# The second layer's modulation summed in one PSUM bank, with the FFN's gating and low parts on GpSimd

## The chip, the cores and the metric

The kernel runs on one core of one Trainium2 chip. The metric is the device time of one execution in microseconds (us), as the median of several runs. The core's engines are TensorE (PE in the profile; PEld is its loading of weights), VectorE (DVE), ScalarE (ACT), GpSimd (POOL) and SyncE (SP), which here issues the DMAs. Each engine works through its own instructions in order, and waits on semaphores for the others.

## What is computed

The reference is one inference step of a small diffusion backbone: two layers, width 1024, with 128 context tokens and 1024 latent tokens. The inner dimension of the FFN is 2816. What matters for this change is the modulation and the FFN:

```python
for i in range(DEPTH):                                   # 2 layers
    mc = split(silu(c_ctx) @ w_mod[i] + b_mod[i], 6)     # context stream
    ml = split(silu(c)     @ w_mod[i] + b_mod[i], 6)     # latent stream
    h  = rmsnorm(x, norm_mix[i]) * (1 + m[1]) + m[0]
    x  = x + m[2] * mixer_i(h)      # layer 0: attention and pooling, layer 1: convolution module
    h  = rmsnorm(x, norm_ffn[i]) * (1 + m[4]) + m[3]
    x  = x + m[5] * conv_ffn(h)

def conv_ffn(h, w_in, conv_w, conv_b, w_out):
    a, g = split(dwconv3(h @ w_in, conv_w, conv_b), 2)
    return (silu(a) * g) @ w_out
```

`m` is `mc` for the context tokens and `ml` for the latent ones. The six modulation vectors of a layer are a product of two vectors of length 1024 with a matrix of 1024 x 6144, 25 MB that are read once and used for very little arithmetic. Everything is in float32.

## The kernel before

**Layout and precision.** Activations stand feature-major: eight tiles `xs[k]` of 128 features by 1154 columns (128 context tokens, 2 of gap, 1024 latent tokens). A large product is made of three matmuls in the faster float32r: each operand is split in a high part and a low part (the value less its high part), and `mm3` adds high x high, high x low and low x high into the same PSUM tile. A weight unit (`wunit`, L242) is a DMA of 512 KB into `wraw`, a high part `whi` by ACT (L252) and a low part `wlo` by Pool (L254). The two raw buffers and the three buffers each of `whi` and `wlo` are used in turn. While layer 0's first FFN part runs, its low parts are also stored in DRAM, and its second part loads them from there.

**Stages.** After attention (`mixer0`) comes `trunk`. The tokens are cut in two parts, about 664 and 492 columns wide, and the stages follow one another so that each part's vector work lies beside the other's matmuls. The wider part takes two matmuls per 128 x 128 weights (332 columns each), the other takes one. The order in `trunk` is:

1. the output projection of layer 0 on part OA (`out_tiles`, eight tiles, the first three together), then on part OB;
2. layer 0's FFN on part FA0, then on part FB0;
3. layer 1's convolution module, beside FB0 and after it;
4. layer 1's FFN on FA1 and FB1.

**What is done beside the matmuls** is written as generators. Each `yield` ends a step, and `pull(q, n)` or `tick(n)` runs steps from the list between the pieces of the main loop. In OA, `pull(mods, MS)` runs four steps of the modulation after each of its six yields. In OB, `tick(3)` runs the norm for FA0, and no modulation (`MT` is 0). In FA0, `tick(MO)` runs 1.1 steps after each yield, first of the norm for the other part (17 steps), then what is left of the modulation. A planner with a timeline of expected times then sets the order of the instructions on each engine, SP and its DMA queue included.

**The modulation of layer 1** (`mod_beside`, L309) is a matrix-vector product for two streams done by DVE, for three groups m of two vectors each. For each of eight row blocks k and each of four column chunks of 512 it loads a tile `mraw` of 256 KB, multiplies it by the stream's 128 scalars (one per partition) and adds it into one of eight accumulators `modacc` in SBUF, four for each stream (L322 for k = 0, L324 for the others). So there are 32 steps of two operations each, one for each stream, and then a step in which eight matmuls with a column of ones (L330) sum over the partitions into the PSUM tile `modps`, and a step in which `mod_spread` (L336) copies it, turns it into columns and adds the bias. That is 34 steps a group, 102 in all. There are eight buffers of `mraw`.

**The FFN** (`ffn`, L1076) goes through 22 pairs of a projection a and a projection g. `conv` (L1087) empties the PSUM tile with a three-tap convolution: ACT (L1091), then DVE twice (L1092, L1094). `pair` then takes the Silu of a, multiplies by g (L1104) and splits the product in high (`fh`, ACT, L1107) and low (`fl`, L1108). After each two pairs `out` (L1112) runs the output projection for eight tiles d, each with a residual add by DVE (L437, in `residual`), in four yields. It runs behind the first pair of the next two. The engine of L1104 and L1108 is chosen by whether a PSUM pool `psd` exists: with it Pool does both, without it DVE does L1108 and, for a part of two chunks, L1104.

**PSUM** has eight banks. From the start of `trunk` until the sixth yield of FB0 the pools are `psum(3, 0, 2)`: three tiles `mm` of two banks and two auxiliary banks. Later stages have the extra pool `psd`, in which the convolution of layer 1 (L996) accumulates.

The norm's chain is: squares by ACT (L402), added by DVE (L406), summed over partitions by TensorE (L380), `rsv` by DVE (L368), the power -1/2 `rsr` by Pool (L371), and a broadcast by TensorE (L392).

Of the kernel before, what the change touches and what calls it, by code (L numbers as in the profile page):

```python
# [9 lines left out]
F32 = mybir.dt.float32  # L10
F32R = mybir.dt.float32r
AF = mybir.ActivationFunctionType
ALU = mybir.AluOpType
# [6 lines left out]
P = 128  # L20
D = 1024
KT = D // P
# [94 lines left out]
FA1, FB1 = Part(0, 648), Part(642, T)  # L117
UW = 692
SIDE_A = 7
MO = 1.1  # L120
MS = 4
MT = 0
MI = 1.1
PF = (1, 3, 2, 0)
SEQ = (0, 0), (0, 1), (1, 0), (1, 1), (2, 0), (2, 1)
KP = 0
# [62 lines left out]
class Kern:  # L189
# [119 lines left out]
    def mod_beside(self, l, m, mp, ev):  # L309

        nc = self.nc
        accs = [mp.tile([P, 512], F32, tag="macc", name=self.nm("modacc")) for _ in range(8)]
        for k in range(KT):
            for u in range(2):
                for x in range(2):
                    rv = mp.tile([P, 512], F32, tag="mraw", name=self.nm("mraw"))
                    o = u * 1024 + x * 512
                    nc.sync.dma_start(rv, self.i["wmod"][l, m, k, :, o:o + 512])
                    for s in range(2):
                        acc, c = accs[4 * s + 2 * u + x], self.sc[:, k, s:s + 1]  # L320
                        if k == 0:
                            i = nc.vector.tensor_scalar(acc, rv, c, None, op0=ALU.mult)  # L322
                        else:
                            i = nc.vector.scalar_tensor_tensor(acc, rv, c, acc, op0=ALU.mult, op1=ALU.add)  # L324
                        self.tc.keep_in_program_order(i)
                    yield
        ps = self.psa.tile([P, 512], F32, tag="aux", name=self.nm("modps"))
        for s in range(2):
            for g in range(4):
                nc.tensor.matmul(ps[32 * g:32 * g + 32, :], self.one[:, 1 - s:33 - s], accs[4 * s + g],  # L330
                                 start=s == 0, stop=s == 1)
        yield
        self.mod_spread(l, m, ps, ev, self.psa, "aux")
        yield
# [911 lines left out]
    def trunk(self):  # L1246
        tc, nc, I, cp = self.tc, self.nc, self.i, self.cp
# [9 lines left out]

        with ExitStack() as st:
            pool = lambda n, b, **kw: st.enter_context(tc.tile_pool(name=n, bufs=b, reuse_waits="tile", **kw))
            self.psum(3, 0, 2)  # L1260
            st.callback(lambda: self.pstack.close())
            xp = pool("xp", 1)
            self.halo = xp.tile([P, KT, 32], F32, name="halo")
# [5 lines left out]
            hB = pool("hB", 16)  # L1269
            nt = pool("nt", 3)  # L1270
            beside = ExitStack()
            mp = beside.enter_context(tc.tile_pool(name="mp", bufs=8, reuse_waits="tile"))
            self.tw = 664
            xs = []
            for k in range(KT):
                x = xp.tile([P, T], F32, name=f"x_{k}")
# [7 lines left out]
            for part, Hc in ((OA, mkA()), (OB, mkB(OB.c0))):  # L1284
                Hc.order = order
                tiles = {}
                for k in order:
                    c = ft.tile([P, self.tw], F32, tag="ft", name=self.nm("cat"))
# [14 lines left out]
            for _ in self.out_tiles(OA, I["woab"], cat[OA], xs, self.mod(0, 2), 0, 664, first=3):  # L1303
                self.pull(mods, MS)
            gf0 = self.gain(0, 4, "nf0")
# [11 lines left out]
            for o in self.ffn(0, FA0, xs, HA, self.mod(0, 5), 0, 662, ft, None):  # L1317
                self.tick(MO if o else MI)
            self.flush(self.bg)
# [8 lines left out]
            accs = []  # L1328
# [30 lines left out]
            accs = []  # L1359
# [145 lines left out]
```

## Time and profile before

| what | us |
|---|---|
| median of three runs | 2699.41 |
| lowest and highest of them | 2694.0, 2701.53 |
| the profiled execution: time | 2696.8 |
| the profiled execution: span of the core | 2694.8 |

The mean granted clock of TensorE was 0.989 of full speed in the profiled execution. The page shows one execution. "Busy" is the time in which an engine ran an instruction of its own, "idle before" is the time that it stood still ahead of one, and "<-" names what it waited for. Row groups give the line of the kernel, the engine, the operation, the output and inputs by the program's names, the shape, the count after "x", and then busy time and mean ns of one. In a timeline, the first number is the start and the second the time from there to the end of the merged pieces; instructions are pipelined, so that the next one of an engine starts before the one ahead of it has wholly ended.

The modulation of layer 1 stands in the trace as 24 operations of L322 and 168 of L324 on DVE, from 541 to 1140 us, and 48 matmuls of L330.

### The profile page before, as it was taken

What the parts mean: (1) busy time and instruction counts of PE and PEld (TensorE: products, weight loads), DVE (VectorE), ACT (ScalarE), POOL (GpSimd) and SP (SyncE); (2) the same over time, 40 slices, a digit from 0 to 9 for tenths busy, and PEclk for the clock granted to TensorE, in tenths of its full rate; (3) what the DMA queues carried; (4) which work ended last, traced back from release to release, by engine and by line L of the source; (5) the groups of instructions that cost most, each with busy time, mean ns of one, the idle gap of its engine ahead of it and who ended that gap; (6) DMA issues with size and microseconds to landing.
All of it is one profiled execution on the core that took longest, in us unless ns stands there. A gap on an engine that the chain in (4) does not pass through costs nothing.

```text
span 2694.8 us, 38615 instructions
## 1 busy us (share of the span) xinstructions
PE 2605.4 (97%) x14982; PEld 2352.9 (87%) x14982; DVE 1597.6 (59%) x2455; ACT 1124.1 (42%) x1743; POOL 1244.9 (46%) x736
## 2 busy tenths in 40 slices
PE   6999998989999999999999999999999999999999
PEld 4698897788999999989998889889999999888887
DVE  6046777493567767654997854379964344444444
ACT  4326666525422222354545364555324323433332
POOL 1322333265433332233556254689757544655553
PEclk9999998999999999999999999999999999999999
DMA  7612235564446555444444553222222222433332
GB/s 283 221 51 79 71 79 142 184 198 135 139 161 205 190 172 179 170 160 141 141 133 133 187 188 102 87 87 76 73 71 71 79 80 70 129 93 95 95 96 89
DMA packets 139734, 345.88 MB, mean 128 GB/s; under 512 B 46112, under 2 KB 51872, under 8 KB 139552
## 3 DMA queue, kind: packets, MB, share of 16 engines
q1 hardware_dynamic: 139552, 343.41, 40.1%
q8 instruction: 119, 1.95, 0.3%
q14 instruction: 63, 0.52, 0.1%
HBM read 291.97 MB, written 46.67 MB: 126 GB/s over the span
## 4 chain that ended last, share of the span: by engine, by line
PE 82%; DVE 10%; ACT 2%; issue 2%; DMA 2%; POOL 1%; SPq 0%; POOLq 0%; DVEq 0%; ACTq 0%
PE mm L264 15%; PE mm L268 15%; PE mm L266 15%; PE mn L264 8%; PE mn L266 8%; PE mn L268 8%; PE mm L454 2%; DVE modacc L324 2%; DVE x L437 2%; PE O L888 2%; DVE dacc L996 1%; PE tp L856 1%; PE qps L638 1%; PE qps L639 1%; PE qps L640 1%
## 5 line engine op out<-in xcount | busy, mean ns | idle before, releaser
L254 POOL TENSOR_TENSOR wlo<-wraw,whi 128x1024 fp32r<-128x1024 f32 x280 | 687.7, 2462 | 909.3 <-ACT whi L252 737.6
L252 ACT ACTIVATE whi<-wraw 128x1024 fp32r<-128x1024 f32 x348 | 364.5, 1057 | 770.8 <-PE mm L266 396.4
L264 PE MATMUL mm<-h,whi 128*128 128x332 f32 (+6 forms) x2208 | 558.3, 323 | 7.1 <-DVE x L437 6.6
L268 PE MATMUL mm<-h,wlo 128*128 128x332 f32 (+6 forms) x2208 | 560.0, 324 | 0.9 <-POOL wlo L254 0.8
L266 PE MATMUL mm<-h,whi 128*128 128x332 f32 (+6 forms) x2208 | 558.6, 324 | 0.0
L264 PEld LDWEIGHTS mm<-h,whi 128*128 128x128 f32 x2208 | 382.6, 189 | 21.5 <-issue 8.6
L268 PEld LDWEIGHTS mm<-h,wlo 128*128 128x128 f32 x2208 | 381.0, 189 | 13.5 <-POOL wlo L254 1.9
L266 PEld LDWEIGHTS mm<-h,whi 128*128 128x128 f32 x2208 | 379.7, 189 | 10.4
L996 DVE SCALAR_TENSOR_TENSOR dacc<-u,params,dacc 128x661 f32<-128x661 f32 (+1 forms) x344 | 285.3, 829 | 7.6
L437 DVE SCALAR_TENSOR_TENSOR x<-mm,mod,x 128x128 f32<-128x128 f32 (+7 forms) x408 | 210.4, 559 | 130.8 <-PE mm L268 129.2
L264 PE MATMUL mn<-h,whi 128*128 128x494 f32 (+1 forms) x672 | 262.5, 391 | 3.2 <-DVE x L437 3.2
L266 PE MATMUL mn<-h,whi 128*128 128x494 f32 (+1 forms) x672 | 262.1, 390 | 0.0
L268 PE MATMUL mn<-h,wlo 128*128 128x494 f32 (+1 forms) x672 | 260.5, 390 | 0.0
L1092 DVE SCALAR_TENSOR_TENSOR facc<-mm,params,facc 128x663 f32<-128x663 f32 (+3 forms) x92 | 82.1, 892 | 275.0 <-ACT facc L1091 274.9
L1092 DVE SCALAR_TENSOR_TENSOR facc<-mn,params,facc 128x493 f32<-128x493 f32 (+1 forms) x84 | 62.0, 738 | 218.6 <-ACT facc L1091 218.5
L264 PE MATMUL mm<-fh,whi 128*128 128x332 f32 (+2 forms) x720 | 171.7, 318 | 14.2 <-DVE x L437 12.3
L268 PE MATMUL mm<-fh,wlo 128*128 128x332 f32 (+2 forms) x720 | 169.5, 315 | 0.0
L266 PE MATMUL mm<-fl,whi 128*128 128x332 f32 (+2 forms) x720 | 169.4, 315 | 0.0
L978 POOL TENSOR_TENSOR acc<-acc,tap 128x508 f32<-128x508 f32 (+1 forms) x104 | 151.3, 1460 | 38.6 <-ACT tap L977 32.6
L1104 POOL TENSOR_TENSOR facc<-facc,facc 128x494 f32<-128x494 f32 (+2 forms) x66 | 91.3, 1383 | 145.1 <-DVE facc L1094 145.1
L437 DVE SCALAR_TENSOR_TENSOR x<-mn,mod,x 128x510 f32<-128x510 f32 (+1 forms) x168 | 120.5, 736 | 63.8 <-PE mn L268 63.0
L1107 ACT ACTIVATE fh<-facc 128x664 fp32r<-128x664 f32 (+3 forms) x88 | 60.2, 684 | 227.5 <-POOL facc L1104 140.1
(227 smaller groups left out, 4539.1 us busy)
## 6 DMA issues: line engine op xcount, KB each, us to landing
wraw<-in_fi_dram SPq DMA_DIRECT2D x176, 512.0 KB
wraw<-in_fo_dram SPq DMA_DIRECT2D x88, 512.0 KB
mraw<-in_wmod_dram SPq DMA_DIRECT2D x48, 512.0 KB
mraw<-in_wmod_dram SPq DMA_DIRECT2D x96, 256.0 KB
wraw<-in_pw_dram SPq DMA_DIRECT2D x48, 512.0 KB
lowi<-wlo SPq DMA_DIRECT2D x44, 512.0 KB
wlo<-lowi SPq DMA_DIRECT2D x44, 512.0 KB
lowo<-wlo SPq DMA_DIRECT2D x22, 512.0 KB
```

Of the source, the lines that this page charges most:

```text
L252: nc.scalar.activation(hi, raw, AF.Copy)
L254: (eng or nc.gpsimd).tensor_tensor(lo, raw, hi.bitcast(F32), op=ALU.subtract)
L264: mm(pv, whi, xhi[:, a:b], start=start, stop=False)
L266: mm(pv, whi, xlo[:, a:b], start=False, stop=False)
L268: mm(pv, wlo, xhi[:, a:b], start=False, stop=stop)
L324: i = nc.vector.scalar_tensor_tensor(acc, rv, c, acc, op0=ALU.mult, op1=ALU.add)
L437: nc.vector.scalar_tensor_tensor(xd[:, a:b], pv, gate[:, d, st:st + 1], xd[:, a:b], op0=ALU.mult, op1=ALU.add)
L978: nc.gpsimd.tensor_tensor(acc[:, :n], acc[:, :n], p[:, :n], op=ALU.add)
L996: nc.vector.scalar_tensor_tensor(acc[:, :n] if t == NCK - 1 else pacc, u[:, t:t + n], wk(i, t), acc[:, :n] if t == side else pacc, op0=ALU ...
L1092: nc.vector.scalar_tensor_tensor(acc[:, 1:W], part.ps(ps, 0, W - 1), w(0), acc[:, 1:W], op0=ALU.mult, op1=ALU.add)
L1104: (nc.gpsimd if side or part.n == 1 else nc.vector).tensor_tensor(a[:, :W], a[:, :W], g[:, :W], op=ALU.mult)
L1107: nc.scalar.activation(hi[:, :W], a[:, :W], AF.Copy)
```

## The change

```diff
-MO = 1.1
-MS = 4
+MO = 1.3
+MS = 2
+MR = 11
 MT = 0
-MI = 1.1
+MI = 1.3
...
     def mod_beside(self, l, m, mp, ev):
 
         nc = self.nc
-        accs = [mp.tile([P, 512], F32, tag="macc", name=self.nm("modacc")) for _ in range(8)]
-        for k in range(KT):
-            for u in range(2):
-                for x in range(2):
-                    rv = mp.tile([P, 512], F32, tag="mraw", name=self.nm("mraw"))
-                    o = u * 1024 + x * 512
-                    nc.sync.dma_start(rv, self.i["wmod"][l, m, k, :, o:o + 512])
-                    for s in range(2):
-                        acc, c = accs[4 * s + 2 * u + x], self.sc[:, k, s:s + 1]
-                        if k == 0:
-                            i = nc.vector.tensor_scalar(acc, rv, c, None, op0=ALU.mult)
-                        else:
-                            i = nc.vector.scalar_tensor_tensor(acc, rv, c, acc, op0=ALU.mult, op1=ALU.add)
+        accs = [mp.tile([P, 512], F32, tag="macc", name=self.nm("modacc"), bufs=8) for _ in range(8)]
+        raws = []
+
+        def load():
+            n = len(raws)
+            if n < 4 * KT:
+                raws.append(mp.tile([P, 512], F32, tag="mraw", name=self.nm("mraw"), bufs=MR))
+                nc.sync.dma_start(raws[n], self.i["wmod"][l, m, n % KT, :, n // KT * 512:n // KT * 512 + 512])
+
+        for _ in range(MR):
+            load()
+        for g in range(4):
+            for s in range(2):
+                acc = self.psd.tile([P, 1, 512], F32, tag="acc", name=self.nm("macc"))[:, 0]
+                for k in range(KT):
+                    rv, c = raws[g * KT + k], self.sc[:, k, s:s + 1]
+                    if k == 0:
+                        nc.scalar.activation(acc, rv, AF.Identity, scale=c)
+                    else:
+                        i = nc.vector.scalar_tensor_tensor(accs[4 * s + g] if k == KT - 1 else acc, rv, c, acc,
+                                                           op0=ALU.mult, op1=ALU.add)
                         self.tc.keep_in_program_order(i)
-                    yield
+                    if s:
+                        load()
+                    if k % 2:
+                        yield
...
-            self.psum(3, 0, 2)
+            self.psum(3, 0, 1, 1)
...
-            mp = beside.enter_context(tc.tile_pool(name="mp", bufs=8, reuse_waits="tile"))
+            mp = beside.enter_context(tc.tile_pool(name="mp", bufs=1, reuse_waits="tile"))
```

- The eight sums of a group m are made one after the other: for each chunk g and each stream s, eight products over k. The running sum is in a PSUM bank of the pool `psd`, of which there is one. The last of the eight writes its result to the accumulator in SBUF, as before.
- The first product of each sum (24 in all) is by ACT, the other seven (168) by DVE.
- A step is two products of one sum, where it was one tile for both streams. There are still 32 such steps in a group, and the two that follow.
- A raw tile is used by both streams, eight products apart. Eleven tiles are loaded ahead, and the next is loaded after each product of the second stream. The 96 loads of 256 KB are the same data in another order, by chunk and not by row block.
- OA gets two steps per yield, 12 in all, and 90 are left for FA0, where 1.3 steps are run per yield.
- `psum(3, 0, 1, 1)` takes one of the two auxiliary banks for `psd`. Since `psd` then exists from the start of `trunk`, the FFN's product (L1104) and low part (L1108) are Pool's for the 22 pairs of FA0, and the low part of the first pair of FB0 as well.

## The prediction

> **What bounds the kernel now.** I read the top of the page first, then the windows cut at the stages that the change touches, then TensorE's waits inside them.
>
> ```profile
> span 2694.8 us, 38615 instructions
> PE 2605.4 (97%) x14982; PEld 2352.9 (87%) x14982; DVE 1597.6 (59%) x2455; ACT 1124.1 (42%) x1743; POOL 1244.9 (46%) x736
> PE 82%; DVE 10%; ACT 2%; issue 2%; DMA 2%; POOL 1%; SPq 0%; POOLq 0%; DVEq 0%; ACTq 0%
> ```
>
> TensorE sets the time: the chain runs through it for 82%. The change removes none of its matmuls, so a gain can only come out of its gaps. The chain also has 10% on DVE, and the next view says where DVE matters.
>
> ```profile
> core 0: us, PE busy (x) PEld busy (x) DVE busy (x) ACT busy (x) POOL busy (x), PEclk, DMA share, GB/s
> 517.00:578.50 61.50, 59.55 (x390) 58.79 (x389) 40.85 (x40) 15.18 (x21) 28.85 (x15) 1.00 0.69 237
> 578.50:640.00 61.50, 51.55 (x222) 43.24 (x221) 36.57 (x51) 27.75 (x49) 40.48 (x17) 0.92 0.47 154
> 640.00:1145.00 505.00, 494.93 (x3196) 482.53 (x3194) 331.28 (x462) 154.11 (x186) 171.30 (x75) 1.00 0.52 173
> ```
>
> The three stretches are the output projection of part OA, that of part OB, and the first FFN part FA0. In the middle one TensorE is busy for 51.55 of 61.50 us, at a granted clock of 0.92. FA0 has 10.07 us of gaps in 505. The waits of TensorE, first for 517 to 640 and then for 640 to 1145, name the cause:
>
> ```profile
> PE mm L264 <- DVE x L437: 6.6, 4, 2.4
> PE mm L392 <- POOL rsr L371: 4.0, 1, 4.0
> PE mm L268 <- POOL wlo L254: 0.8, 2, 0.5
> ```
>
> ```profile
> PE mm L264 <- DVE x L437: 10.0, 7, 2.1
> ```
>
> L437 is the residual add, which empties a PSUM tile and so frees it for the next matmuls. DVE reaches it late. The timeline of DVE in OA shows why:
>
> ```profile
> 541.44 11.77 DVE L322 TENSOR_SCALAR modacc<-mraw,sc 128x512 f32<-128x512 f32 x8
> ...
> 587.27 8.66 DVE L324 SCALAR_TENSOR_TENSOR modacc<-mraw,sc,modacc 128x512 f32<-128x512 f32 x8
> 595.85 0.84 DVE L406 TENSOR_TENSOR sq<-sq,sq 128x664 f32<-128x664 f32 x1
> 596.62 1.02 DVE L437 SCALAR_TENSOR_TENSOR x<-mm,mod,x 128x128 f32<-128x128 f32 x2
> ```
>
> Behind each tile's residual (the last row, two pieces) stand eight modulation operations, 8.66 and 11.77 us in the batches shown. A tile of OA takes TensorE 48 matmuls of 0.153 us (59.55 us in 390), 7.3 us. The queue falls behind in OA and is still paying in OB.
>
> **The change part by part.** *Fewer steps in OA.* Two steps for four per yield leaves a tile with one residual (1.02 us), one square add (0.84) and four modulation operations for eight. At 1.25 us a step (worked out below) these are 2.5 us, so 4.4 us in all, under the 7.3 us of the matmuls. DVE no longer trails, and what it held up in OB falls away:
>
> ```profile
> 587.50 0.46 PE L264 MATMUL mm<-h,whi 128*128 128x490 f32 x1 [1.47 <-DVE x L437]
> ...
> 590.41 0.61 PE L264 MATMUL mm<-h,whi 128*128 128x490 f32 x1
> 590.82 0.61 PE L266 MATMUL mm<-h,whi 128*128 128x490 f32 x1
> ...
> 593.23 0.38 PE L264 MATMUL mm<-h,whi 128*128 128x490 f32 x1
> 593.45 0.38 PE L266 MATMUL mm<-h,whi 128*128 128x490 f32 x1
> ```
>
> The terms: residual waits 6.6, a late low part 0.5 of the 0.8. Then the clock: soon after a wait the matmuls start every 0.41 us (590.41 to 590.82) where they start every 0.22 otherwise (593.23 to 593.45). The window's 0.92 on 61.5 us is some 4.9 us of clock, of which I count 3.0 for the two spells before 605 (eight matmuls each, 0.19 us too long). Together 10.1 us.
>
> The wait of 4.0 us for rsr is the same backlog by another way:
>
> ```profile
> 599.51 8.79 POOL L254 TENSOR_TENSOR wlo<-wraw,whi 128x1024 fp32r<-128x1024 f32 x2 [7.44 <-ACT whi L252]
> 611.83 2.35 POOL L254 TENSOR_TENSOR wlo<-wraw,whi 128x1024 fp32r<-128x1024 f32 x1 [3.53 <-ACT whi L252]
> 614.13 1.32 POOL L371 TENSOR_TENSOR rsr<-rsv,mhalf 128x6 f32<-128x6 f32 x1
> ```
>
> Two low parts take 8.79 us on Pool against 2.35 for one, while DVE runs the modulation. The next low part comes late by its high part (3.53), and rsr stands behind it in Pool's queue. With DVE idle there, I drop this wait too: 4.0. OA and OB give **14.1 us**.
>
> *The sums into PSUM.* From the per-line answers, with minimum, median and maximum in ns:
>
> ```profile
> L324 DVE SCALAR_TENSOR_TENSOR modacc<-mraw,sc,modacc x168: 732/743/2914, 555.8 to 1139.4; 128x512 f32<-128x512 f32 x168
> L996 DVE SCALAR_TENSOR_TENSOR dacc<-u,params,dacc x344: 734/898/912, 1267.3 to 1987.2; 128x661 f32<-128x661 f32 x88, 128x508 f32<-128x508 f32 x84
> L996 DVE SCALAR_TENSOR_TENSOR dacc<-u,params,acc x16: 868/1860/3050, 1265.3 to 1959.8; 128x661 f32<-128x661 f32 x8, 128x508 f32<-128x508 f32 x8
> ```
>
> The convolution's sums (L996) already accumulate in PSUM and never pass 912 ns, though Pool is often busy beside them; with both inputs in SBUF (acc) the same line reaches 3050, as the modulation reaches 2914. So the stretched ones go. The price is order: the new sums depend on each other. Six dependent PSUM sums take 4.68 us in the convolution, (4.68 - 0.74)/5 = 0.79 from start to start, against 0.66 for the independent ones now (the four from 832.48 to 835.13, below). A step of two then costs 1.45 (one dependent start, one covered by other work) for 1.32, and with the first of each eight on ACT 1.25 on average.
>
> ```profile
> 1860.84 4.68 DVE L996 SCALAR_TENSOR_TENSOR dacc<-u,params,dacc 128x508 f32<-128x508 f32 x6
> ```
>
> Both have 0.73 as the least, so the place itself is charged at nothing. The Trainium skill speaks against that (Perfetto Trace Analysis, Optimizing Scalar/DVE Operations): it charges DVE about 125 ns of access on PSUM and 60 on SBUF. By it each sum would cost 0.065 us more, an estimate, 0.6 us for the ten of an out section, and the sum would be 10 us for 16; the least of 732 and 734 ns doesn't bear it out.
>
> *Gating and low parts on Pool.* They leave DVE and come back slower on Pool (rows of FA0, then of the later FA1, 640:1145 and 1790:2280):
>
> ```profile
> L1104 DVE TENSOR_TENSOR facc<-facc,facc 128x664 f32<-128x664 f32 x22 | 19.3, 878 | 0.4
> L1108 DVE TENSOR_TENSOR fl<-facc,fh 128x664 fp32r<-128x664 f32 x22 | 18.6, 845 | 9.9 <-ACT fh L1107 9.9
> L1108 POOL TENSOR_TENSOR fl<-facc,fh 128x648 fp32r<-128x648 f32 x20 | 33.6, 1682 | 6.9 <-ACT fh L1107 6.9
> L1104 POOL TENSOR_TENSOR facc<-facc,facc 128x648 f32<-128x648 f32 x21 | 33.5, 1594 | 11.2 <-DVE facc L1094 11.2
> ```
>
> DVE sheds 37.9 us. Pool takes about 22 x (1.59+1.68) = 72 us on its 171 of 505, still under half. A pair's product reaches its matmuls about 1.6 us later, behind at least one more projection of 7.3 us, and FA1 runs so already: nothing charged. If that cover went, it would be 1.6 us a pair.
>
> *FA0's out sections.* Here is one, ending in a wait of 2.05 us at 836.30:
>
> ```profile
> 827.76 0.84 DVE L1104 TENSOR_TENSOR facc<-facc,facc 128x664 f32<-128x664 f32 x1
> 828.52 1.96 DVE L437 SCALAR_TENSOR_TENSOR x<-mm,mod,x 128x128 f32<-128x128 f32 x4
> ...
> 831.72 0.84 DVE L1108 TENSOR_TENSOR fl<-facc,fh 128x664 fp32r<-128x664 f32 x1
> 832.48 2.73 DVE L324 SCALAR_TENSOR_TENSOR modacc<-mraw,sc,modacc 128x512 f32<-128x512 f32 x4
> 835.13 1.96 DVE L437 SCALAR_TENSOR_TENSOR x<-mm,mod,x 128x128 f32<-128x128 f32 x4
> ```
>
> ```profile
> 836.30 0.54 PE L264 MATMUL mm<-fh,whi 128*128 128x332 f32 x2 [2.05 <-DVE x L437]
> ```
>
> No row of DVE there shows an idle time ahead of it. Gate and low part free 0.76 each, from their starts to the next rows': 1.5. A section has four yields, so 4.4 steps now and 5.2 after: 6.5 us (at 1.25) for 5.8 (at 1.32), plus 0.7. A wait of 2 shrinks by 0.8, in about six sections of ten (10.0 us in 7 waits): 5 gained. Against it stands the **hand-over**, which the trace does not show: the first product of each sum is on ACT, needs the one bank free (the last DVE sum of the chain before), and the second waits on DVE for it. Queued behind it on DVE stand the residuals, and behind the product on ACT the high parts of weights and facc. Of 24 such, some ten fall into out sections. Nothing, where DVE has other work; at most about 1.8, a weight conversion ahead of it (1.06) and the product (near the 0.76 of the activation fh):
>
> ```profile
> L252 ACT ACTIVATE whi<-wraw 128x1024 fp32r<-128x1024 f32 x67 | 69.8, 1056 | 207.2 <-PE mm L266 131.8 <-DMA wraw<-in_fi_dram 67.1 <-PE mm L268 8.1
> ```
>
> ```profile
> 828.63 0.76 ACT L1107 ACTIVATE fh<-facc 128x664 fp32r<-128x664 f32 x1 [5.74 <-DVE facc L1104]
> ```
>
> I take 0.3 each, 3 us, as ACT is busy 154 of 505. FA0 nets 2.
>
> *At nothing:* one auxiliary bank for two (the spread needs its copy first anyway). Eleven raw tiles ahead for eight: 3 x 256 KB at 237 GB/s is 3.3 us of transfer, once, beside tiles of 7.3; if weights stood behind it, 0 to 3 us. The loads, their number and SP's queue are otherwise as they were, each behind the DVE operation that frees its tile.
>
> **Sum:** 14.1 + 2 = 16 us. The profiled execution took 2696.8 us (span 2694.8, 2.0 around it), 2.6 below the median of the runs shown, 2699.41: 2696.8 - 16 = **2681**.
>
> **The rivals.** *Half of it (same).* The waits on L437 in OA and OB go, 6.6, but rsr still stands behind a weight's low part and the clock spells stay in part, and FA0 loses 2 to hand-overs: about 2692. For it: Pool's queue order is planned ahead, and rsr's wait is on Pool. A form of it is the port: the Trainium skill, same page and section, says that Pool and DVE share a port, so that moving work between them might not help. As a mechanism here: if the PSUM sums were held up by Pool's 72 us more, at FA0's present mean of 0.911 for 0.743, ten sums cost 1.7 us a section, its six waits come to 2.9 each and the other four to 0.9, so FA0 loses 9 and the hand-overs' 3: 2695.
>
> ```profile
> L324 DVE SCALAR_TENSOR_TENSOR modacc<-mraw,sc,modacc 128x512 f32<-128x512 f32 x128 | 111.1, 911 | 0.0
> ```
>
> L996's maximum of 912 speaks against it.
>
> *Slower.* The product is queued on ACT behind fh. That instruction already waits 5.74 us in the section shown, and now waits for Pool: gate 1.59, fh 0.76, product 0.76, so DVE stands up to 3.1 us with the residuals behind it. With 3.1 - 0.8 = 2.3 in each of ten sections FA0 loses 23; less the 14.1 won before it, or the 6.6 alone, that is 2706 to 2713. It decides from 1.4 us per section. Against it: ACT is idle two thirds of FA0, and orders are planned by expected times.
>
> *All of it.* No gap and no slow clock is left in the three stretches: 1.95 in OA, 9.95 and 4.9 in OB, 10.07 in FA0, 27 in all: 2670.
>
> **How the numbers follow.** Forecast (2673 to 2690) 0.50, all of it 0.14, half of it 0.19 (0.05 of it the port), slower 0.17. A measurement of this kernel tells about 0.3%, 8 us, from no change. Faster by more than that 0.64; within it 0.22, as the low end of the slower rival (0.03) lies there; slower 0.14. The range for 8 in 10 reaches from 2667, just past the rival that takes all, to 2708, into the slower one.
>
> **What would show it.** Right: no wait on L437 from 570 to 600, a clock of 1.00 and about 47 us for OB (61.5 less 9.95 and 4.9), rsr within 2 us of rsv, no modulation sum over 1 us, waits in FA0's out sections of about 1 us. Wrong: DVE waiting for ACT's products by more than 1 us each, ACT's weight conversions behind them, L437 waits over 10 us in FA0, or TensorE waiting for fl or wlo on Pool. The engines' planned orders can also shift work that the diff does not touch, in either direction; the range holds a few us for it.

## The result, and the profile after

The changed kernel takes 2670.24 us (median of four runs, 2666.9 to 2672.02) beside 2699.49 for the kernel before on the same chip: a ratio of 0.9892, 95% interval 0.9879 to 0.9906, or 29 us. The forecast, 2681, was 18 below it. The page of the profiled execution (span, busy time, and the chain by engine):

```profile
span 2670.2 us, 38723 instructions
PE 2604.2 (98%) x14982; PEld 2352.7 (88%) x14982; DVE 1507.0 (56%) x2386; ACT 1139.3 (43%) x1767; POOL 1303.8 (49%) x781
PE 90%; DVE 5%; DMA 2%; ACT 1%; POOL 1%; issue 1%; SPq 0%; POOLq 0%; DVEq 0%; ACTq 0%
```

TensorE's busy time is nearly what it was (2605.4). The chain runs through PE for 90% where it was 82%: what it passes through has moved from other engines to PE, and the gain itself is 1% of the time. The windows of the same three stretches, with the columns of before:

```profile
517.00:578.50 61.50, 60.08 (x400) 59.16 (x400) 32.64 (x46) 21.35 (x31) 30.40 (x16) 1.00 0.73 258
578.50:640.00 61.50, 61.50 (x327) 55.69 (x326) 27.45 (x35) 33.37 (x61) 38.33 (x19) 1.00 0.38 117
640.00:1145.00 505.00, 505.00 (x3243) 487.75 (x3242) 285.21 (x441) 169.64 (x203) 231.48 (x117) 1.00 0.54 180
```

TensorE has no gap left from 578.5 to 1145, and the clock of the second window is 1.00 for 0.92. In TensorE's waits from 517 to 640 the residual and rsr no longer stand:

```profile
PE O L895 <- DVE ptl L873: 0.6, 1, 0.6
PE mm L265 <- DVE ao L911: 0.5, 1, 0.5
PE mm L269 <- POOL wlo L255: 0.4, 1, 0.4
```

For the comparison of kernels I take three lengths from TensorE's timelines: OA from its first matmul to the first of OB (the first 490-column one), OB from there to the first 332-column one of FA0, and FA0 from there to the first matmul into `mn` in FB0. Here are the two marks of the changed kernel's OB, its first matmul and FA0's:

```profile
581.90 0.38 PE L265 MATMUL mm<-h,whi 128*128 128x490 f32 x1
...
627.08 0.47 PE L265 MATMUL mm<-h,whi 128*128 128x332 f32 x2
```

| us | OA | OB | FA0 | sum |
|---|---|---|---|---|
| before | 63.0 | 59.4 | 523.3 | 645.7 |
| after | 59.9 | 45.2 | 513.2 | 618.3 |

So 27.4 us come from the stretch that the change touches: 3.1, 14.2 and 10.1. Outside it the two profiles differ by 3 us the other way; OA starts at 522.0 for 517.5, but at anything from 514.1 to 522.8 in the profiles below, whose code ahead of OA is the same.

### The profile page after: what moved, and what is told of

Read it like the earlier page. It is cut to its first block, busy times and chain, and to the rows that moved or that the text cites. A ratio compares the mean times of both kernels' runs of the same rounds, so it can differ in the third digit from the quotient of the medians.

```text
span 2670.2 us, 38723 instructions
## 1 busy us (share of the span) xinstructions
PE 2604.2 (98%) x14982; PEld 2352.7 (88%) x14982; DVE 1507.0 (56%) x2386; ACT 1139.3 (43%) x1767; POOL 1303.8 (49%) x781
## 4 chain that ended last, share of the span: by engine, by line
PE 90%; DVE 5%; DMA 2%; ACT 1%; POOL 1%; issue 1%; SPq 0%; POOLq 0%; DVEq 0%; ACTq 0%
PE mm L265 17%; PE mm L269 17%; PE mm L267 17%; PE mn L265 8%; PE mn L267 8%; PE mn L269 8%; PE mm L466 2%; PE O L900 2%; PE qps L650 1%; PE qps L651 1%; PE tp L868 1%; PE qps L652 1%; DVE dacc L1008 1%; PE modps L304 1%; PE vps L622 1%
## 5 line engine op out<-in xcount | busy, mean ns | idle before, releaser
L255 POOL TENSOR_TENSOR wlo<-wraw,whi 128x1024 fp32r<-128x1024 f32 x280 | 675.1, 2416 | 797.1 <-ACT whi L253 776.7
L1104 DVE SCALAR_TENSOR_TENSOR facc<-mm,params,facc 128x663 f32<-128x663 f32 (+3 forms) x92 | 82.1, 892 | 305.6 <-ACT facc L1103 305.4
L1116 POOL TENSOR_TENSOR facc<-facc,facc 128x664 f32<-128x664 f32 (+3 forms) x88 | 126.8, 1441 | 152.3 <-DVE facc L1106 152.3
L1104 DVE SCALAR_TENSOR_TENSOR facc<-mn,params,facc 128x493 f32<-128x493 f32 (+1 forms) x84 | 62.0, 738 | 217.3 <-ACT facc L1103 217.3
```

The source lines that it names most:

```text
L255: (eng or nc.gpsimd).tensor_tensor(lo, raw, hi.bitcast(F32), op=ALU.subtract)
L1104: nc.vector.scalar_tensor_tensor(acc[:, 1:W], part.ps(ps, 0, W - 1), w(0), acc[:, 1:W], op0=ALU.mult, op1=ALU.add)
L1116: (nc.gpsimd if side or part.n == 1 else nc.vector).tensor_tensor(a[:, :W], a[:, :W], g[:, :W], op=ALU.mult)
```

## The experiments

Three accounts stood against each other. The **queue account** is the prediction's: DVE's work per tile falls, by the smaller batches in OA and by Pool's part and the PSUM sums in FA0. The **pace account** puts all of it on the step rates. The **order account** puts FA0's gain on where the sums stand among the residuals. All kernels computed the whole step; each label's lengths are in the table at the end of this section.

### One part alone, in the kernel before

`e1_pace`: the new step rates.

```diff
-MO = 1.1
-MS = 4
+MO = 1.3
+MS = 2
...
-MI = 1.1
+MI = 1.3
```

> The kernel before with the new pace alone (two steps per yield in OA, 1.3 in FA0). Queue account (the gain of OA and OB is the smaller batch behind each residual; that of FA0 is the shorter work of DVE per section): TensorE's waits on the residual between OA and FA0 fall from 6.6 us to under 1, OB takes 45 to 48 us for 59, but FA0's waits grow from 10 us to 13 to 20, as each out section gets 5.2 steps for 4.4: 2685 to 2692 in all. Rival, pace account (the pace is all of it): FA0's waits fall too, 2670 to 2675.

Measured: 2682.06 us, ratio 0.9939 (0.9927 to 0.9951). OA and OB are at once as short as in the changed kernel. FA0 is not: TensorE's residual waits from 505 to 1140 are

```profile
PE mm L264 <- DVE x L437: 11.5, 7, 3.0
```

and FA0 takes 525.1 us, 1.8 longer than before. The waits grew by 1.5 us where the queue account had 3 to 10, and the time lies below its range. The pace gives OA and OB, and costs a little in FA0, as the queue account said, though less than it said.

`e2_gate_pool`: the product and low part of FA0 on Pool.

```diff
-            side = self.psd is not None
+            side = self.psd is not None or part is FA0
```

> The kernel before with FA0's product and low part on Pool alone. Queue account: nothing changes in OA and OB; in FA0 each out section loses 1.5 us of DVE work, so that waits of 2 us fall to 0.5 and the 10 us to 2 to 4: 2691 to 2694. Rival, order account (what frees FA0 is that the dependent sums are put one at a time between the residuals, not the amount of work): the waits of FA0 stay at 8 to 10 us: 2697 to 2700.

Measured: 2706.53 us, ratio 1.0029 (1.0017 to 1.0041): slower, which neither account had. FA0 takes 8.7 us longer than before: TensorE's gaps there are 14.5 us for 10.1, and the other 4.3 us lie outside them, 1.7 of these in a second spell at half clock (3.4 us from 839.7). In one of its out sections DVE and Pool do this (the timelines of DVE, then of Pool):

```profile
1067.17 0.90 DVE L1094 SCALAR_TENSOR_TENSOR facc<-mm,params,facc 128x663 f32<-128x663 f32 x1
1067.98 5.45 DVE L324 SCALAR_TENSOR_TENSOR modacc<-mraw,sc,modacc 128x512 f32<-128x512 f32 x4
1073.35 1.02 DVE L437 SCALAR_TENSOR_TENSOR x<-mm,mod,x 128x128 f32<-128x128 f32 x2
1074.29 1.40 DVE L324 SCALAR_TENSOR_TENSOR modacc<-mraw,sc,modacc 128x512 f32<-128x512 f32 x2
```

```profile
1068.21 2.01 POOL L1104 TENSOR_TENSOR facc<-facc,facc 128x664 f32<-128x664 f32 x1 [1.23 <-DVE facc L1094]
1071.09 1.79 POOL L1108 TENSOR_TENSOR fl<-facc,fh 128x664 fp32r<-128x664 f32 x1 [0.87 <-ACT fh L1107]
```

Four sums stand in a row ahead of a residual, and as Pool works just then, they take 5.45 us where four took 2.73 before (at 832.48 in the prediction's rows). In the seven out sections that are counted below DVE runs 60 sums for 57, little more than before, but at a mean of 994 ns for 733, or 59.7 us for 41.8. These 18 us are more than the 1.5 us a section, 10.5 in seven, that Pool's part took off DVE. The groups of the sums from 640 to 1145 show it as a mean, first for this kernel, then for `e4_sbuf_sum` and the changed kernel (the last row's sums are in PSUM):

```profile
L324 DVE SCALAR_TENSOR_TENSOR modacc<-mraw,sc,modacc 128x512 f32<-128x512 f32 x124 | 134.8, 1131 | 0.0
```

```profile
L332 DVE SCALAR_TENSOR_TENSOR modacc<-mraw,sc,modacc 128x512 f32<-128x512 f32 x147 | 153.9, 1055 | 1.4
```

```profile
L332 DVE SCALAR_TENSOR_TENSOR macc<-mraw,sc,macc 128x512 f32<-128x512 f32 x126 | 94.5, 750 | 5.9 <-ACT macc L330 4.5
```

The mean was 911 ns before. The Trainium skill has this as a rule (SBUF — State Buffer, section SBUF: two separate sides): a DVE operation with two SBUF inputs and a GpSimd operation that reads SBUF exclude each other for the whole instruction. The runs agree: 1131 ns with Pool's added work, and 750 with one input in PSUM and about as much of Pool beside it.

`e8_pace_gate`: both of the above.

```diff
-MO = 1.1
-MS = 4
+MO = 1.3
+MS = 2
...
-MI = 1.1
+MI = 1.3
...
-            side = self.psd is not None
+            side = self.psd is not None or part is FA0
```

> The kernel before with the new pace and Pool's product and low part, but the sums still in SBUF, two streams at a time. Queue account: OA and OB as in the changed kernel, FA0's waits 4 to 8 us (5.2 steps for 4.4, 1.5 us less of other work, sums still stretched where Pool runs): 2675 to 2680. Order account: FA0's waits stay near 10 us or above: 2681 to 2686. If the PSUM sums add nothing: 2670.

Measured: 2685.9 us, ratio 0.9951 (0.9938 to 0.9964), and FA0 at 532.8 us with residual waits of 17.4: the order account's figures. The pace and Pool's part together leave out just what made FA0 better.

`e11_raw11`: eleven raw buffers.

```diff
-        accs = [mp.tile([P, 512], F32, tag="macc", name=self.nm("modacc")) for _ in range(8)]
+        accs = [mp.tile([P, 512], F32, tag="macc", name=self.nm("modacc"), bufs=8) for _ in range(8)]
...
-                    rv = mp.tile([P, 512], F32, tag="mraw", name=self.nm("mraw"))
+                    rv = mp.tile([P, 512], F32, tag="mraw", name=self.nm("mraw"), bufs=11)
```

> The kernel before with eleven raw buffers for eight and nothing else. Order account: DVE's order is as before, so the waits of 6.6, 4.0 and 10 us stay: 2695 to 2702. Rival (SP's queue is blocked by raw tiles and that is what delays weights and rsr): the 4.0 us wait for rsr goes and OB is 5 us shorter or more: 2688 to 2694.

Measured: 2697.22 us, ratio 0.9998 (0.9988 to 1.0008). More buffers alone change nothing.

### One part taken out of the changed kernel

`e3_gate_dve`: FA0's product and low part back on DVE.

```diff
-            side = self.psd is not None
+            side = self.psd is not None and part is not FA0
```

> The changed kernel with FA0's product and low part back on DVE. Queue account: 1.5 us more of DVE work in each out section, FA0's waits from 0 to 3 to 8 us: 2674 to 2680; OA and OB as changed. Order account: the residuals still stand between single sums, FA0's waits stay under 2 us: 2669 to 2672.

`e4_sbuf_sum`: the running sum in SBUF.

```diff
-                acc = self.psd.tile([P, 1, 512], F32, tag="acc", name=self.nm("macc"))[:, 0]
+                acc = accs[4 * s + g]
...
-                        i = nc.vector.scalar_tensor_tensor(accs[4 * s + g] if k == KT - 1 else acc, rv, c, acc,
+                        i = nc.vector.scalar_tensor_tensor(acc, rv, c, acc,
```

> The changed kernel with each running sum in its SBUF accumulator, in the same order and pace, so that only the place of the sum differs. Place account (a DVE operation with both inputs in SBUF stands still while Pool runs): the 168 sums of DVE take 0.9 to 1.1 us on average for 0.75, some of them over 2 us, and Pool's low parts are stretched as well; TensorE waits 3 to 10 us in FA0: 2674 to 2682. Rival (the order alone matters): sums stretched, but with one at a time between the residuals no wait: 2669 to 2672.

`e5_first_dve`: the first product on DVE.

```diff
-                        nc.scalar.activation(acc, rv, AF.Identity, scale=c)
+                        i = nc.vector.tensor_scalar(acc, rv, c, None, op0=ALU.mult)
...
-                        self.tc.keep_in_program_order(i)
+                    self.tc.keep_in_program_order(i)
```

> The changed kernel with the first product of each sum on DVE too, so that there is no hand-over. Account of the prediction (hand-overs cost FA0 some 3 us): 2667 to 2670, and DVE's waits for the product (4.5 us in 7) go. Rival (they are hidden, as DVE waits for ACT only 4.5 us and TensorE not at all): within 2 us of the changed kernel, 2669 to 2672; 24 more DVE operations of about 0.5 to 0.75 us make it no slower by more than that.

`e7_twice`: the first product four times over on ACT.

```diff
-                        nc.scalar.activation(acc, rv, AF.Identity, scale=c)
+                        for _ in range(4):
+                            nc.scalar.activation(acc, rv, AF.Identity, scale=c)
```

> The changed kernel with ACT making each first product four times over, so that each hand-over takes some 1.9 us longer (three more activations at 0.62). The prediction's slower rival decides from 1.4 us per section: by it the ten or so hand-overs in out sections bring waits of TensorE of 5 to 20 us, 2676 to 2690. If the hand-overs have cover: 2670 to 2673, with DVE waiting 30 to 45 us for the products and TensorE under 2.

`e6_old_pace`: the old step rates.

```diff
-MO = 1.3
-MS = 2
+MO = 1.1
+MS = 4
...
-MI = 1.3
+MI = 1.1
```

> The changed kernel with the old pace (four steps per yield in OA, 1.1 in FA0). Queue account: a tile of OA has 1.02 + 0.84 + 4 x 1.25 = 6.9 us of DVE work for 7.3 us of matmuls, so DVE just keeps up: waits of 0 to 3 us in OA and OB, none in FA0: 2670 to 2675. Pace account (OA and OB gain by the pace alone): the waits of 6.6 and 4.0 us and the clock come back in OB: 2682 to 2687.

Measured, with the ratios to the kernel before: 2670.51 (0.9894; 0.9882 to 0.9907), 2668.8 (0.9898; 0.9883 to 0.9912), 2667.76 (0.9895; 0.988 to 0.9909), 2670.14 (0.9905; 0.989 to 0.9919) and 2670.73 us (0.9899; 0.9883 to 0.9916). **None of the four parts taken out is needed while the others are there**, and a long hand-over costs nothing. All five intervals hold the changed kernel's 0.9892. `e3_gate_dve` came out as the order account had it. `e5_first_dve` has a time in the range of the prediction's hand-overs, but not by them: FA0 takes 513.2 us with the hand-overs and without them, and the 2.5 us lie outside the three stages.

In `e4_sbuf_sum` the sums are stretched to 1055 ns, as the place account expected, and yet TensorE doesn't wait in FA0. In `e7_twice` the hand-over is made long, seen in ACT's and DVE's waits at it:

```profile
  DVE modacc L333: 47.1, 18
  ACT macc L331: 14.8, 6
```

ACT stands 47.1 us for the bank and DVE 14.8 us for ACT, against 49.5 and 4.5 in the changed kernel, and TensorE notices neither. DVE's wait was expected at 30 to 45 us, so the hand-over was made longer by less than was meant.

`e6_old_pace` came out as the queue account had it, and against the pace account: with four steps per yield OA and OB stay at 59.9 and 45.2 us. Its windows, and below them those of `e9_order_only`, which has the same pace and the same order, but sums in SBUF and all on DVE:

```profile
517.00:578.50 61.50, 60.65 (x398) 60.08 (x398) 39.29 (x55) 21.31 (x30) 30.46 (x16) 1.00 0.83 289
578.50:640.00 61.50, 61.50 (x328) 55.76 (x327) 32.37 (x42) 37.03 (x66) 38.67 (x20) 1.00 0.51 166
```

```profile
517.00:578.50 61.50, 59.42 (x390) 58.22 (x387) 40.55 (x40) 16.27 (x25) 30.26 (x15) 1.00 0.67 236
578.50:640.00 61.50, 48.08 (x209) 40.84 (x208) 42.58 (x53) 22.62 (x31) 28.39 (x14) 0.89 0.49 150
```

So OA and OB have two remedies, and either is enough: a smaller batch (`e1_pace`), or the new sums of the changed kernel at the old batch. The timelines of DVE and Pool show what the new sums do there. First `e9_order_only`, then `e6_old_pace`:

```profile
589.75 1.02 DVE L449 SCALAR_TENSOR_TENSOR x<-mm,mod,x 128x128 f32<-128x128 f32 x2
591.09 1.41 DVE L332 SCALAR_TENSOR_TENSOR modacc<-mraw,sc,modacc 128x512 f32<-128x512 f32 x2
592.65 2.84 POOL L255 TENSOR_TENSOR wlo<-wraw,whi 128x1024 fp32r<-128x1024 f32 x1 [6.27 <-ACT whi L253]
593.17 5.65 DVE L332 SCALAR_TENSOR_TENSOR modacc<-mraw,sc,modacc 128x512 f32<-128x512 f32 x5
598.74 1.03 DVE L449 SCALAR_TENSOR_TENSOR x<-mm,mod,x 128x128 f32<-128x128 f32 x2
```

```profile
572.77 1.03 DVE L449 SCALAR_TENSOR_TENSOR x<-mm,mod,x 128x128 f32<-128x128 f32 x2
579.66 1.03 DVE L449 SCALAR_TENSOR_TENSOR x<-mm,mod,x 128x128 f32<-128x128 f32 x2
584.38 2.40 POOL L255 TENSOR_TENSOR wlo<-wraw,whi 128x1024 fp32r<-128x1024 f32 x1 [2.97 <-ACT whi L253]
585.10 3.92 DVE L332 SCALAR_TENSOR_TENSOR macc<-mraw,sc,macc 128x512 f32<-128x512 f32 x5
```

From one tile's residual to the next DVE takes 8.99 us in `e9_order_only`, more than TensorE's 7.3 for a tile, and 6.89 in `e6_old_pace`, less than that and as expected. Of these 2.1 us, 1.7 are the five sums: beside one low part of Pool they take 5.65 us in SBUF and 3.92 in PSUM. The first product on ACT saves about 0.4 (590.69 to 591.09 on DVE). Pool's product and low part have no share in it, as `e2_gate_pool` leaves OA and OB as they were.

### The order of the sums

`e9_order_only`: the kernel before with the new order and loads, and nothing else (sums in SBUF, as in `e4_sbuf_sum`, first product on DVE, as in `e5_first_dve`, `MR = 11`). The lines are against the changed kernel; the old step rates and `psum(3, 0, 2)` are back as well.

```diff
         for g in range(4):
             for s in range(2):
-                acc = self.psd.tile([P, 1, 512], F32, tag="acc", name=self.nm("macc"))[:, 0]
+                acc = accs[4 * s + g]
                 for k in range(KT):
...
-                        nc.scalar.activation(acc, rv, AF.Identity, scale=c)
+                        i = nc.vector.tensor_scalar(acc, rv, c, None, op0=ALU.mult)
```

> The kernel before with the new order of the sums alone (one stream's chunk after the other, each operation on the result of the one ahead of it, eleven raw tiles), in SBUF, all on DVE, with the old pace, the old banks, and the product and low part on DVE. Order account (DVE's instructions are planned so that single dependent sums stand between the residuals): OB's and FA0's waits go as in the changed kernel, the stretch from OA to FB0's first two-bank-free matmuls is 618 to 622 us, 2668 to 2674 in all. If another part of the change is needed beside it: 630 us or more, 2682 to 2692.

Measured: 2690.39 us, ratio 0.9965 (0.9952 to 0.9977). The second case's figures came (639.0 us from OA to the end of FA0), but by OB alone: FA0 is cured, 513.3 us, and OB is worse than before, 63.7. TensorE's waits from 517 to 640:

```profile
PE mm L404 <- POOL rsr L383: 7.0, 1, 7.0
PE mm L265 <- DVE x L449: 6.5, 3, 3.6
```

`e10_two_streams` is the changed kernel with both streams per tile again, the sums in SBUF and all on DVE; `e13_two_before` is the kernel before with the same loop, by chunk and with the loads ahead. Both have this loop:

```diff
+        for g in range(4):
+            for k in range(KT):
+                for s in range(2):
+                    acc = accs[4 * s + g]
+                    rv, c = raws[g * KT + k], self.sc[:, k, s:s + 1]
+                    if k == 0:
+                        i = nc.vector.tensor_scalar(acc, rv, c, None, op0=ALU.mult)
+                    else:
+                        i = nc.vector.scalar_tensor_tensor(acc, rv, c, acc, op0=ALU.mult, op1=ALU.add)
+                    self.tc.keep_in_program_order(i)
+                load()
+                yield
```

> The changed kernel with the two streams' sums side by side again: a step is one raw tile for both streams, two operations that do not depend on each other, in SBUF on DVE; chunk order, pace, loads ahead, banks and Pool's part as changed. Dependence account (it is the dependence within a sum that spaces the operations): pairs stand ahead of residuals again, FA0's waits are 4 to 12 us, 2674 to 2682. Rival (the order by chunk and the loads ahead do it): no waits, 2667 to 2671.

> The kernel before with the order by chunk and the loads ahead, but two streams side by side; pace, banks, engines as before. Dependence account: as the kernel before, FA0's waits 8 to 15 us and OB's backlog as before, 2692 to 2700. Rival (chunk order and loads ahead): 2668 to 2675. Between them: part of the gain comes from tiles that are ready earlier.

Measured: 2675.97 us, ratio 0.9909 (0.9896 to 0.9923), and 2688.97 us, ratio 0.9956 (0.9943 to 0.9968). The first lies in the range of the dependence account, with waits just below it; the second lies between its two cases. With two streams at the new pace FA0 takes 519.0 us and has small waits:

```profile
PE mm L265 <- DVE x L446: 3.3, 6, 1.0
```

At the old pace it takes 514.8 and has next to none (0.2 us). So the order by chunk with its loads ahead takes most of FA0's waits away, and summing one stream after the other takes the rest where more steps are run (5.8 us between `e10_two_streams` and `e4_sbuf_sum`, which also differ in the engine of the first product, worth nothing in `e5_first_dve`). That it is the dependence which spaces the sums is not shown. In SBUF a sum that needs the one just ahead of it starts 0.67 us after it (the two of 591.09 above), and the independent sums of the kernel before start every 0.66, so DVE does not wait for the result.

Why, is seen in an out section. First the kernel before, then the changed one, by DVE's timeline:

```profile
1061.08 1.40 DVE L324 SCALAR_TENSOR_TENSOR modacc<-mraw,sc,modacc 128x512 f32<-128x512 f32 x2
1062.41 0.84 DVE L1108 TENSOR_TENSOR fl<-facc,fh 128x664 fp32r<-128x664 f32 x1
1063.17 2.73 DVE L324 SCALAR_TENSOR_TENSOR modacc<-mraw,sc,modacc 128x512 f32<-128x512 f32 x4
1065.82 1.96 DVE L437 SCALAR_TENSOR_TENSOR x<-mm,mod,x 128x128 f32<-128x128 f32 x4
```

```profile
817.24 1.03 DVE L449 SCALAR_TENSOR_TENSOR x<-mm,mod,x 128x128 f32<-128x128 f32 x2 [0.80 <-PE mm L269]
818.19 0.75 DVE L332 SCALAR_TENSOR_TENSOR macc<-mraw,sc,macc 128x512 f32<-128x512 f32 x1
819.06 1.03 DVE L449 SCALAR_TENSOR_TENSOR x<-mm,mod,x 128x128 f32<-128x128 f32 x2
820.01 0.74 DVE L332 SCALAR_TENSOR_TENSOR macc<-mraw,sc,macc 128x512 f32<-128x512 f32 x1
820.89 1.03 DVE L449 SCALAR_TENSOR_TENSOR x<-mm,mod,x 128x128 f32<-128x128 f32 x2
```

Before, six sums and a low part stand between the residual ahead and that of 1065.82, and the residuals of two tiles (four pieces) are then owed together. Now one sum stands between two residuals, and at 817.24 it is DVE that waits for TensorE. The table takes the last seven sections with the modulation. It gives the most sums that stand on DVE between one residual and the next, then the sums that start between the first and the last matmul on `fh` of a section, and then TensorE's residual waits in all seven:

| kernel | most sums between two residuals | sums in the section | waits, us |
|---|---|---|---|
| before | 6, 6, 4, 2, 4, 6, 6 | 9, 9, 8, 4, 9, 9, 9 | 10.0 |
| e2_gate_pool | 4, 4, 2, 2, 2, 4, 4 | 10, 10, 8, 4, 8, 10, 10 | 14.3 |
| e13_two_before | 3, 3, 3, 2, 3, 4, 4 | 7, 7, 8, 4, 8, 8, 8 | 0.2 |
| e9_order_only | 2, 1, 2, 2, 2, 2, 2 | 6, 5, 6, 4, 6, 6, 6 | 0 |
| after | 1, 1, 1, 1, 1, 1, 2 | 5, 7, 6, 6, 7, 7, 7 | 0 |

In the kernel before, the sections with six sums in a row have waits of 2.0 to 2.1 us, those with four 0.7 and 1.1, and the one with two has none. The number of sums in a section does not decide it: `e13_two_before` has up to 8 and hardly waits. Its rows of three and four cost next to nothing, so the length of the row is not the whole account either. In `e2_gate_pool` the rows are shorter than before, but its sums are the stretched ones.

| us | OA | OB | FA0 |
|---|---|---|---|
| e1_pace | 59.9 | 45.2 | 525.1 |
| e2_gate_pool | 63.0 | 59.2 | 532.0 |
| e8_pace_gate | 59.9 | 45.2 | 532.8 |
| e11_raw11 | 62.9 | 59.3 | 523.4 |
| e3_gate_dve | 59.9 | 45.2 | 513.3 |
| e4_sbuf_sum | 59.9 | 45.2 | 513.2 |
| e5_first_dve | 59.9 | 45.2 | 513.2 |
| e7_twice | 59.9 | 45.2 | 513.2 |
| e6_old_pace | 59.9 | 45.2 | 514.6 |
| e9_order_only | 62.0 | 63.7 | 513.3 |
| e10_two_streams | 59.9 | 45.2 | 519.0 |
| e13_two_before | 66.2 | 56.8 | 514.8 |

No version could beat the changed kernel in this stretch by less DVE work: in 45.2 and 513.2 us TensorE is busy without a break, and in OA's 59.9 it stands 0.9 us, for `ao` and a low part.

## Why the prediction was right, and where it was wrong

The direction was right, and 2670.24 lies in the range from 2667 to 2708. But it lies below the forecast's own 2673 to 2690: it is the time of the rival "all of it", 2670, which had a chance of 0.14. For OA and OB only a size was off. For FA0 the mechanism was wrong, and it is luck that its gain, too small by 8 us, left the time inside the range. Step by step:

- **OA and OB, 14.1 us: the mechanism was right, the size too small.** 17.3 came. `e1_pace` shows that the smaller batch alone does it, rsr's wait included, so that this wait was DVE's backlog as argued. The waits themselves came to the 11.1 us that were counted. The mis-sized term is the clock: the kernel before has three spells at half clock in OB, 3.4 us each, and the prediction counted the first two, 3.0 us. The third begins 0.6 us after the end of the wait for rsr (615.50). Three spells at half clock are 5.1 us. The rest, 1.1 us, was put at nothing: each of the six waits costs about 0.2 us more than its gap, as matmuls otherwise start before the one ahead has ended. From 578.42 to 580.49 are 2.07 us, 1.76 more than the usual 0.31, for a gap of 1.60. Here are the windows of the three spells, with the clock third from the end, and then the two rows of TensorE, all of the kernel before:

```profile
588.80:592.20 3.40, 3.40 (x9) 2.79 (x10) 3.40 (x3) 0.35 (x1) 2.85 (x1) 0.50 0.64 199
599.00:602.40 3.40, 3.40 (x10) 2.79 (x9) 3.40 (x6) 1.49 (x2) 2.89 (x1) 0.50 0.69 232
616.10:619.50 3.40, 3.40 (x16) 3.17 (x15) 1.11 (x2) 0.22 (x1) 1.66 (x1) 0.50 0.49 136
```

```profile
578.42 0.47 PE L268 MATMUL mm<-h,wlo 128*128 128x332 f32 x2
580.49 0.46 PE L264 MATMUL mm<-h,whi 128*128 128x490 f32 x1 [1.60 <-DVE x L437]
```

In Pool's timeline rsr now follows 2.1 us after rsv (599.19 on DVE):

```profile
598.91 2.40 POOL L255 TENSOR_TENSOR wlo<-wraw,whi 128x1024 fp32r<-128x1024 f32 x1 [2.88 <-ACT whi L253]
601.27 1.32 POOL L383 TENSOR_TENSOR rsr<-rsv,mhalf 128x6 f32<-128x6 f32 x1
```

- **The PSUM sums: right that the stretched ones go, and without effect at the new pace.** None is over 759 ns (before: 2914). With the sum in SBUF the time is the same (`e4_sbuf_sum`). They count where Pool is busy and the batch is large, in OB at the old pace: they are 1.7 of the 2.1 us by which a tile is shorter in `e6_old_pace` than in `e9_order_only`. The price of 0.79 us from start to start came, but its reason was half wrong. Dependence alone does not cost it, as dependent sums in SBUF start every 0.67 us (`e9_order_only`). PSUM alone does not cost it either: behind the PSUM sum of 545.93 in the changed kernel an operation that does not need it starts 0.66 later. The 0.13 more is paid where a sum reads from PSUM what the one just ahead of it wrote, so the place was not free, as the prediction had it from the least times of 732 and 734 ns.

```profile
L332 DVE SCALAR_TENSOR_TENSOR macc<-mraw,sc,macc x144: 742/748/759, 545.9 to 1099.5; 128x512 f32<-128x512 f32 x144
```

- **FA0, 2 us: wrong, 10.1 came.** The step that failed is "A section has four yields, so 4.4 steps now and 5.2 after". What is yielded in a section is not what DVE runs there. By that step DVE has 8.8 sums in a section before and 9.1 after (one product in eight is ACT's); it ran 8.1 and 6.4 on average. And a wait does not go by the work in a section: it goes with the sums that stand in a row ahead of a residual, up to six before, one or two after, and that changed with the order of the sums (`e9_order_only`).
- **The gate and the low part, 1.5 us freed per section: wrong.** In the old order Pool's part costs FA0 8.7 us (`e2_gate_pool`), as it stretches the sums in SBUF by more than it frees; in the new one it is worth nothing (`e3_gate_dve`). The port rival feared such a cost for the PSUM sums; it fell on sums in SBUF only.
- **The hand-over, 3 us: nothing.** Without it (`e5_first_dve`) and with four products for one (`e7_twice`) the time is the same. The slower rival didn't come about, as no such wait on DVE exceeds 0.8 us in the changed kernel:

```profile
DVE macc L332 <- ACT macc L330: 4.5, 7, 0.8
```

- **At nothing:** right for the raw buffers (`e11_raw11`) and, by FA0's and OB's full speed, for the auxiliary bank.

What stays open: the order by chunk and the loads issued ahead of use were not tried apart, and the planner's expected times, which turn the new order into single sums between residuals, are not seen in a trace. In `e9_order_only` the backlog in OB is that of the stretched sums, but its wait for rsr is 7.0 us for 4.0 before. Ahead of it ACT waits 9.74 us for a weight (`wraw`, landed at 615.8), and why that came late is not shown. Nor is it why OA takes 66.2 us in `e13_two_before`.

## What to carry to other kernels

When a wait for an emptied PSUM tile is laid at an engine's door, count what stands in that engine's queue ahead of the emptying instruction before counting how busy the engine is: six sums in a row ahead of it cost 2 us of TensorE, and about as many in the same section, spread one to a tile, cost nothing. Taking work off such an engine by giving it to GpSimd can lose more than it frees: here DVE's operations with two SBUF inputs went from a mean of 911 to 1131 ns. Change the order first, on its own, and measure parts both alone and by taking them out: here four of them are each dispensable, and one of those, alone, is a loss.

## What the runs showed of the hardware that was not expected

- Waits of TensorE cost more than themselves in OB: with 8.4 us of gaps, four waits of 0.5 to 4.0 us, OB was 14.2 us longer than without. Of the other 5.9 us, 5.1 are three spells at half clock, 3.4 us each, that begin 0.1, 1.2 and 0.6 us after the end of a wait.
- A DVE sum that reads from PSUM what the sum just ahead of it wrote starts 0.79 us after it; with the sum in SBUF, or with an operation that does not need the result, it is 0.66 to 0.67.
- ACT stood 49.5 us for the single PSUM bank (47.1 us with the product made four times), and nothing that TensorE needs came late.
- The time ahead of OA, under code that no kernel here changed, varied by 8.7 us between profiles (514.1 to 522.8), which is more than several of the effects measured. The lengths of the stages repeat to 0.2 us wherever TensorE has no gap.
